# A hybrid decoder layer on one Trainium2 core: the second dilated pair and branch a take the logits of two query groups in one visit

## The chip, the cores and the metric

One core of one Trainium2 chip runs the whole layer. The metric is the device time of one execution in microseconds, the median of several runs. TensorE multiplies matrices into PSUM, of which the kernel uses eight banks; VectorE (DVE), ScalarE (ACT) and GpSimd (POOL) work on vectors; SyncE (SP) issues most of the loads. The program gives each engine its own list of instructions, which wait for those of other engines through semaphores.

## The reference

One layer, 256 tokens of width 1024, all float32. Three attention branches read one projection of x, and their outputs are merged under sigmoid gates:

```python
o_a = dsa_mixer(...)      # 6 heads share one key and value head; top-64 keys per query by an indexer
o_b = dilated_mixer(...)  # 3 query groups of 4 heads over shared keys and values
o_c = moba_mixer(...)     # 6 heads, causal within the one block of 256
gates = jax.nn.sigmoid(x @ w_gate[i]).reshape(bsz, s_len, N_BRANCH, D_MODEL)
merged = (gates[:, :, 0] * (o_a @ w_br_a[i]) + gates[:, :, 1] * (o_b @ w_br_b[i])
          + gates[:, :, 2] * (o_c @ w_br_c[i]))
x = layer_norm(ALPHA * x + merged @ w_out[i], ln1_g[i], ln1_b[i])
h = jnp.square(jax.nn.relu(x @ w_up[i])) @ w_down[i]
ple = jax.nn.sigmoid(x @ w_ple_gate[i]) * (p[i] @ w_ple[i])
x = layer_norm(ALPHA * x + h + ple, ln2_g[i], ln2_b[i])
```

Every head is softmax(q·k + bias + mask) times v. The bias is a table by distance; in branch a the mask comes from the top-64 selection.

## The kernel before

Float32 products are made of three matmuls: each operand is split into a high part of a shorter format and a low rest, and hi·hi, hi·lo and lo·hi are summed in PSUM (`prod`, line 189). For weights, `Weights._split` loads a unit into a `raw` buffer (SP), ACT casts its high part `whi` (line 112), DVE and POOL subtract to get `wlo` (lines 119 and 123). Buffers of `raw` and of the parts are five each, and units are split four ahead of their use, so a weight that is cast late also makes a later load late.

The first half of the program, up to about 198 us, computes the three branches. Its work is cut into units that the code interleaves:

- `feat(f)` makes 128 columns of queries or keys (24 matmuls of 128x256); `q_pair` and `k_pair` take the result out of PSUM.
- `fill("g")` makes one gate unit: 24 matmuls of 128x256 into a bank of the pool `mm` (three banks), then ACT's tanh at line 311 takes it out to `G`, and the bank is free.
- `fill("c")` makes one merge unit of branches b and c: 15 matmuls into an `mm` bank that read `op[:, 3..7]`, the outputs of five head pairs, then three DVE instructions (lines 326 and 327). A merge unit that lacks the output of one head pair keeps its bank until that output is there.
- `logits(k, *qs)` (line 347) makes the scores of the two heads of a query group: 12 matmuls that contract over 64 rows, the two heads on the two halves of the array, into one bank of `b0`, `b1`, `b2` for each head. Called with two groups, it makes 24 matmuls and takes four banks, the fourth being `b3` (`ps_t`), which the transposes of `attend` use otherwise. Before the change the first dilated pair and the indexer call it so.
- `head` (branches a and c) adds the bias and finds the row's extreme on DVE (line 416, two instructions, 128 and 256 columns), exps on ACT (line 419, two, each with a read of the accumulator), a reciprocal (DVE) and two scalings (ACT, line 408), then `attend`: three transposes on TensorE (line 388), two copies of the result (ACT line 389, DVE 390), two matmuls P·V (lines 392 and 393), ACT's copy `ov` (396), DVE's `ov` and `o` (397, 398). After the second head of a pair, `pair_out` casts the output to `op` (ACT 401, DVE 402).
- `slots` is the same for the three query groups of a dilated pair, with one softmax over all three.

Branch a has six heads in three pairs (j = 0, 1, 2). Before, each pair had its own q unit, its own logits visit and then its two heads one after the other; for each head POOL adds the bias table T and the selection mask `am` into `ta` (lines 584 and 585). Behind branch a come the last gate and merge units (`fill("gggcc")`), then the merge units of branch a, `merge(p)`, which read `op[:, 0..2]`. The list `TASKS` sets the order in which weight units are loaded and split. A scheduler orders the instructions within each engine from what the code says, so the same edit moves rows on all engines.

Of the kernel before, what the change touches and what calls it, by code (L numbers as in the profile page):

```python
# [11 lines left out]
F32 = mybir.dt.float32  # L12
F32R = mybir.dt.float32r
ALU = mybir.AluOpType
# [16 lines left out]
GONE = -3e38  # L31
# [10 lines left out]


TASKS = ("4 va 5 g 6 7 g 8 g g 9 g 10 11 g 12 g g vb g 13 14 g g 15 16 g g 17 18 g g "
         "19 g c 20 g c g c 21 g c g c g c g g g c c a a a a o o o o").split()


class Apart:
# [95 lines left out]
def hybrid_layer(ctx: ExitStack, tc: tile.TileContext, x0, xn, pT, wqk, wva, wvb, wg, wbc, wba,  # L144
                 wout, wup, wdn, wpg, wple, lnrow, rel, onehot, pick, out):
    nc = tc.nc
    pe, act, dve, pool = nc.tensor, nc.scalar, nc.vector, nc.gpsimd
# [17 lines left out]
    ps_s, ps_t, ps_v, ps_a = turns((0, 1, 2)), turns((3,)), turns((4,)), turns((0, 1, 3, 2, 4))  # L165
# [12 lines left out]
    t = banks.tile([128, 512], F32, name="b4", tag="b4")  # L178
# [28 lines left out]
    right = lambda n, b: one.enter_context(tc.tile_pool(name=n, bufs=b, side="right"))  # L207
# [23 lines left out]
    for t in TASKS:  # L231
# [4 lines left out]
        elif t in "gcao":  # L236
            u, w, n = {"g": (u_g, wg, 1024), "c": (u_bc, wbc, 640), "a": (u_ba, wba, 768),
                       "o": (u_out, wout, 1024)}[t]
# [26 lines left out]
    QC = (slice(0, 128), slice(128, 384))  # L265
# [16 lines left out]
    def q_pair(ps, scale=-0.125):  # L282

        q = qpool.tile([128, 2, S], F32R, name="q", tag="q")
        i = (act.mul(q[:, 0], ps, scale),
             dve.scalar_tensor_tensor(q[:, 1], ps, scale, q[:, 0].bitcast(F32), op0=ALU.mult,
                                      op1=ALU.subtract))
        freed(*i)
        last[:] = (x.ins for x in i)
        return q  # L290
# [38 lines left out]
    def feat(f):  # L329
        ps = mmbank(256)  # L330
        gemm(ps, u_q[f], xs)
        if f > 8:
            next(side, None)
        return ps

    def logits(k, *qs):


        ss = [next(ps_s if n < 3 else ps_t)[:, 0:384] for n in range(2 * len(qs))]
        with tc.high_priority(offset=500):  # L340
            for b in range(2):
                c = slice(b * 128, (b + 1) * 128)
                for n, q in enumerate(qs):
                    for i, (x, y) in enumerate(((1, 0), (0, 0), (0, 1))):
                        for h in (1, 0):
                            d = slice(64 * h, 64 * h + 64)
                            m = pe.matmul(ss[2 * n + h][:, QC[b]], lhsT=q[d, x, c],  # L347
                                          rhs=k[d, y, 0:128 * (b + 1)], start=i == 0, stop=i == 2)
                            if b or n or i or not h:
                                tc.keep_in_program_order(m)  # L350
        return ss
# [48 lines left out]
    def pair_out(o, kt):  # L400
        act.copy(op[:, kt, 0], o)
        dve.tensor_tensor(op[:, kt, 1], o, op[:, kt, 0].bitcast(F32), op=ALU.subtract)
# [5 lines left out]
            act.mul(P[:, QC[b]], P[:, QC[b]], r[:, b:b + 1])  # L408


    def head(s, t0, t1, vh, o, h):
        e = wk.tile([128, 384], F32, name="e", tag="e")
        mx = sm.tile([128, 2], F32, name="mx", tag="mx")
        den = sm.tile([128, 2], F32, name="den", tag="den")
        for b, t in enumerate((t0, t1)):
            dve.tensor_tensor_reduce(e[:, QC[b]], s[h][:, QC[b]], t, op0=ALU.add, op1=ALU.min,
                                     scale=1.0, scalar=-GONE, accum_out=mx[:, b:b + 1])
        for b in range(2):
            act.activation(e[:, QC[b]], e[:, QC[b]], AF.Exp, bias=mx[:, b:b + 1], scale=-1.0,
                           accum_out=den[:, b:b + 1])  # L420
        scale_rows(e, den)
        attend(e, vh, o, h)

    def slots(qs, k, Ts, vh, o, adds, two):

        es = [wk2.tile([128, 3, 384], F32, name="eb", tag="eb") for _ in range(2)]
        mxs = [sm.tile([128, 2, 3], F32, name="mxb", tag="mxb") for _ in range(2)]
        for g in range(3):

            if two and g == 0:  # L430
                s = logits(k, qs[1], qs[0])
                s, ss = s[2:], s[:2]
            else:
                s = ss if two and g == 1 else logits(k, qs[g])
            for h in range(2):
                for b, t in enumerate((Ts[h][:, g, 128:256], Ts[h][:, g, :])):
                    dve.tensor_tensor_reduce(es[h][:, g, QC[b]], s[h][:, QC[b]], t, op0=ALU.add,
                                             op1=ALU.min, scale=1.0, scalar=-GONE,
                                             accum_out=mxs[h][:, b, g:g + 1])
        for h in range(2):  # L440
            e = es[h]
            m = sm.tile([128, 2], F32, name="mx", tag="mx")
            den = sm.tile([128, 2], F32, name="den", tag="den")
            dve.tensor_reduce(m, mxs[h], axis=AX.X, op=ALU.min)
            for b in range(2):
                act.activation(e[:, :, QC[b]], e[:, :, QC[b]], AF.Exp, bias=m[:, b:b + 1],
                               scale=-1.0, accum_out=den[:, b:b + 1])
            adds.tensor_tensor(e[:, 0], e[:, 0], e[:, 1], op=ALU.add)
            adds.tensor_tensor(e[:, 0], e[:, 0], e[:, 2], op=ALU.add)
            scale_rows(e[:, 0], den)  # L450
            attend(e[:, 0], vh + h, o, h)
# [16 lines left out]
    with ExitStack() as begin:  # L468
# [7 lines left out]
        with tc.high_priority(offset=1000):  # L476
            for k in range(KT):
                for i, (a, b) in enumerate(cut[k]):
                    e = nc.scalar if i else nc.sync
                    e.dma_start(g0[:, k, a:b], x0[k, :, a:b])  # L480
            for k in range(KT):
                act.copy(xh[:, k], g0[:, k, 0:S])
                for a, b in cut[k]:
                    a = max(a, S)
# [7 lines left out]
                    pe.matmul(first[f], lhsT=w[:, k, 128 * f:128 * f + 128], rhs=x[:, k],  # L492
                              start=k == i == 0, stop=k == KT - 1 and i == 2)
        iq = [q_pair(ps, 0.125) for ps in first]
    tp, wk, wk2, sm = (right(n, b) for n, b in (("tp", 3), ("wk", 3), ("wk2", 2), ("sm", 6)))
    tab = bias_table()
    ps = feat(4)
    kI, kA = k_pair(ps[0:64], ps[0:64]), k_pair(ps[64:128], ps[64:128])
# [7 lines left out]

    values(u_va, 328, 0, 5, True)
    for j in range(4):
        s = s[2:] if j % 2 else logits(kI, iq[j], iq[j + 1])
        r = wk2.tile([128, 768], F32, name="ri", tag="eb")  # L510
        r = r.rearrange("p (h k) -> p h k", h=2)
        for h in range(2):
            act.activation(r[:, h], s[h], AF.Relu)
            n = 2 * j + h
            dve.scalar_tensor_tensor(idx[:, QC[1]], r[:, h, QC[1]], iw[:, 1, n:n + 1],
                                     idx[:, QC[1]], op0=ALU.mult, op1=ALU.add)
            act.mul(r[:, h, QC[0]], r[:, h, QC[0]], iw[:, 0, n:n + 1])  # L517
            pool.tensor_tensor(idx[:, QC[0]], idx[:, QC[0]], r[:, h, QC[0]], op=ALU.add)
# [14 lines left out]
    def opair():  # L533
        return wk2.tile([128, S], F32, name="o", tag="o")

    for j in range(2):
        ps = feat(5 + 4 * j)
        k = k_pair(ps)
        fill("g")
        qs = []  # L540
        for g in range(3):
            qs.append(q_pair(feat(6 + 4 * j + g)))
            if g:
                fill("g")
        o = opair()
        Ts = [toeplitz(6 + 2 * j + h, 4) for h in range(2)]
        slots(qs, k, Ts, 1 + 2 * j, o, (pool, dve)[j], j == 0)
        pair_out(o, 3 + j)
        banks_first[0] = True
        fill("g")  # L550
# [6 lines left out]
    for j in range(3):  # L557
        ps = feat(13 + 2 * j)
        k = k_pair(ps)
        q = q_pair(feat(14 + 2 * j))  # L560
        s = logits(k, q)
        o = opair()
        for h in range(2):
            n = 2 * j + h
            if n % 3 == 0:
                T = toeplitz(18 + n, 1)
            head(s, T[:, n % 3, 128:256], T[:, n % 3], 5 + n, o, h)
            fill("g")
        pair_out(o, 5 + j)

    for _ in side:
        pass
    T = None
    q = q_pair(feat(19))
    for j in range(3):
        s = logits(kA, q)
        o = opair()
        for h in range(2):
            n = 2 * j + h
            if n % 3 == 0:  # L580
                T = toeplitz(n, 1)
            ta = wk.tile([128, 384], F32, name="ta", tag="ta")
            with tc.issue_after(W.subs[-3]):
                pool.tensor_tensor(ta[:, 0:128], T[:, n % 3, 128:256], am[:, 0:128], op=ALU.add)
                pool.tensor_tensor(ta[:, 128:384], T[:, n % 3], am[:, 128:384], op=ALU.add)
            head(s, ta[:, 0:128], ta[:, 128:384], 0, o, h)
            if h and j < 2:
                q = q_pair(feat(20 + j))
            fill("gc")
        pair_out(o, j)  # L590
    fill("gggcc")
    W.after = ()

# [160 lines left out]
    for i in range(4):  # L754
# [3 lines left out]
        b, cs = i // 2, H[i % 2]  # L758
        t = slice(b * 128, (b + 1) * 128)
# [64 lines left out]
    for k in (*SEQ, *LATE):  # L824
        i = PAIRS.index(k) if k in PAIRS else -1
        n = 512 if i < 0 else 1792
# [11 lines left out]
    wr, wt = {}, {}  # L838
# [287 lines left out]
```

## Time and profile before

| what | value |
|---|---|
| runs of the kernel | 429.45 us median of 3 (429.26, 429.45, 430.65) |
| the profiled execution | 428.66 us |
| its span | 426.9 us |
| granted TensorE clock | 0.998 |
| instructions | 7810 |
| DVE busy | 351.1 us (82%) |
| POOL busy | 118.9 us (28%) |
| HBM read and written | 81.88 MB and 1.90 MB, 196 GB/s over the span |

The page gives each engine's busy time, the chain of work that ended last and the costliest groups; other views give single instructions with their start, duration and the wait ahead of them, or the busy time in a stretch of the span. Matmuls are pipelined: the record of a 128x256 matmul is some 0.28 us long, while one starts every 0.11 us, so costs on TensorE are read from start to start.

### The profile page before, as it was taken

How to read it: one execution, taken by the hardware profiler on the slowest of the kernel's cores; microseconds unless marked ns; L12 is line 12 of the kernel's file. 1: busy time of each engine (PE TensorE's matmuls, PEld its weight loads, DVE VectorE, ACT ScalarE, POOL GpSimd, SP SyncE). 2: the span in 40 equal slices, each digit the busy share in tenths (PEclk: the TensorE clock that was granted, in tenths of full speed). 3: DMA queues.
4: the chain of work that ended last, by engine and by line, in shares of the span. 5: the costliest groups of instructions: out<-in, count | busy, mean ns of one | idle time of the engine just before them, and what ended most of it. 6: DMA issues, size and time to landing. Idle time of an engine off the chain costs nothing.

```text
span 426.9 us, 7810 instructions
## 1 busy us (share of the span) xinstructions
PE 417.1 (98%) x2804; PEld 378.1 (89%) x2804; DVE 351.1 (82%) x645; ACT 279.6 (65%) x531; POOL 118.9 (28%) x127
## 2 busy tenths in 40 slices
PE   8999999999999999999999999999999999999993
PEld 8989999999999999999887888888888888788883
DVE  5968758898676689879967889989998798999755
ACT  6777385585888777858414668887888666567310
POOL 1668474173544556500010002242220000000001
PEclk9999999999999999999999999999999999999999
DMA  8895966567463327587851776785665376646402
GB/s 294 301 327 161 286 222 189 164 201 269 130 181 126 131 63 259 145 267 276 292 206 49 236 257 197 210 291 191 187 207 152 117 266 216 190 147 230 164 2 99
DMA packets 28157, 84.30 MB, mean 197 GB/s; under 512 B 2977, under 2 KB 6985, under 8 KB 27733
## 3 DMA queue, kind: packets, MB, share of 16 engines
q1 hardware_dynamic: 26880, 79.54, 57.0%
q10 hardware_dynamic: 1140, 4.19, 2.8%
q8 instruction: 22, 0.36, 0.4%
q14 instruction: 19, 0.15, 0.1%
q0 software_dynamic: 96, 0.06, 0.0%
HBM read 81.88 MB, written 1.90 MB: 196 GB/s over the span
## 4 chain that ended last, share of the span: by engine, by line
PE 78%; DVE 5%; DMA 4%; issue 2%; ACT 2%; SPq 0%; POOLq 0%; DVEq 0%; POOL 0%; ACTq 0%
PE mm L189 34%; PE b L189 19%; PE mm L891 14%; PE mm L893 7%; DMA xr<-in_wdn_dram 4%; PE b L347 2%; DVE wlo L119 2%; PE b L388 1%; PE b L392 1%; ACT whi L112 1%; DVE Y L853 1%; ACT ri L517 1%; PE b L393 0%; DVE wlo L123 0%; DVE st L701 0%
## 5 line engine op out<-in xcount | busy, mean ns | idle before, releaser
L112 ACT CAST whi<-raw 128x1024 fp32r<-128x1024 f32 (+3 forms) x92 | 89.9, 988 | 38.2 <-PE b L189 14.7
L123 DVE TENSOR_TENSOR wlo<-raw,whi 128x256 fp32r<-128x256 f32 (+3 forms) x118 | 96.4, 840 | 16.6 <-ACT whi L112 13.9
L189 PE MATMUL mm<-xh,whi 128*128 128x256 f32 x336 | 90.2, 280 | 0.0
L189 PE MATMUL mm<-xl,whi 128*128 128x256 f32 x336 | 88.1, 278 | 0.0
L123 POOL TENSOR_TENSOR wlo<-raw,whi 128x384 fp32r<-128x384 f32 (+1 forms) x50 | 68.4, 1377 | 70.2 <-ACT whi L112 65.5
L189 PE MATMUL mm<-xh,wlo 128*128 128x256 f32 x336 | 80.6, 281 | 0.2 <-DVE k L299 0.2
L189 PEld LDWEIGHTS mm<-xh,whi 128*128 128x128 f32 x336 | 63.1, 188 | 0.8
L891 PE MATMUL mm<-x,whi 128*128 128x512 f32 x256 | 63.4, 389 | 0.0
L189 PEld LDWEIGHTS mm<-xl,whi 128*128 128x128 f32 x336 | 63.1, 188 | 0.1
L189 PEld LDWEIGHTS mm<-xh,wlo 128*128 128x128 f32 x336 | 57.8, 188 | 0.8 <-DVE k L299 0.4
L189 PE MATMUL b<-whi,store 128*128 128x512 f32 x168 | 54.1, 389 | 0.0
L891 PEld LDWEIGHTS mm<-x,whi 128*128 128x128 f32 x256 | 45.7, 188 | 7.5
L119 DVE TENSOR_TENSOR wlo<-raw,whi 128x1024 fp32r<-128x1024 f32 (+2 forms) x38 | 43.2, 1159 | 3.7 <-ACT whi L112 3.6
L708 POOL TENSOR_TENSOR rs<-rs,half 128x1 f32<-128x1 f32 x4 | 3.4, 843 | 147.5 <-DVE rs L707 147.5
L110 ACT CAST whi<-raw 128x256 fp32r<-128x256 f32 x64 | 36.9, 617 | 10.0 <-PE mm L891 5.4
L189 PEld LDWEIGHTS b<-whi,store 128*128 128x128 f32 x168 | 31.5, 188 | 6.4
L893 PEld LDWEIGHTS mm<-x,wlo 128*128 128x128 f32 x256 | 33.8, 188 | 2.5
L893 PE MATMUL mm<-x,wlo 128*128 128x256 f32 x256 | 34.2, 276 | 0.0
L189 PE MATMUL b<-wlo,store 128*128 128x512 f32 x84 | 32.8, 391 | 0.3 <-DVE wlo L119 0.3
L914 POOL TENSOR_TENSOR a<-a 128x128 f32<-128x128 f32 x7 | 5.3, 757 | 61.5 <-ACT a L877 55.6
L189 PE MATMUL mm<-op,whi 128*128 128x256 f32 x128 | 22.4, 280 | 0.0
L189 PE MATMUL b<-whi,x 128*128 128x512 f32 x64 | 20.5, 395 | 0.0
(223 smaller groups left out, 824.2 us busy)
## 6 DMA issues: line engine op xcount, KB each, us to landing
raw<-in_wup_dram SPq DMA_DIRECT2D x32, 512.0 KB
raw<-in_wg_dram SPq DMA_DIRECT2D x24, 512.0 KB
raw<-in_wqk_dram SPq DMA_DIRECT2D x18, 512.0 KB
raw<-in_wdn_dram SPq DMA_DIRECT2D x18, 512.0 KB
raw<-in_wout_dram SPq DMA_DIRECT2D x8, 512.0 KB
raw<-in_wpg_dram SPq DMA_DIRECT2D x8, 512.0 KB
T<-tabd SPq DMA_DIRECT2D x24, 128.0 KB
xr<-in_wdn_dram SPq DMA_DIRECT2D x6, 512.0 KB
```

What stands on the lines that cost most here:

```text
L110: i = nc.scalar.copy(blocks(hi, a, b), blocks(r, a, b))
L112: i = nc.scalar.copy(hi, r)
L119: i = e.tensor_tensor(lo[:, x], r[:, x], hi[:, x].bitcast(F32), op=ALU.subtract)
L123: i = e.tensor_tensor(blocks(lo, *x), blocks(r, *x), blocks(hi, *x).bitcast(F32), op=ALU.subtract)
L189: i = pe.matmul(ps, lhsT=a[x], rhs=b[y], start=first and n == 0, stop=last and n == 2, skip_group_check=more)
L347: m = pe.matmul(ss[2 * n + h][:, QC[b]], lhsT=q[d, x, c], rhs=k[d, y, 0:128 * (b + 1)], start=i == 0, stop=i == 2)
L388: pe.transpose(t[:, 128 * i:128 * i + 128], P[:, 128 * i:128 * i + 128], ident)
L392: pe.matmul(v, lhsT=V[:, 0, vh], rhs=pt[:, :, 0:256], start=True, stop=False)
L517: act.mul(r[:, h, QC[0]], r[:, h, QC[0]], iw[:, 0, n:n + 1])
L891: pe.matmul(ps, lhsT=hi[:, c], rhs=x1[:, :, k], start=k == 0, stop=False)
L893: pe.matmul(ps[:, :, 0], lhsT=lo[:, c], rhs=x1[:, :, k, 0], start=False, stop=k == KT - 1)
L914: pool.tensor_tensor(sums[2], a11, a21, op=ALU.subtract)
```

## The change

The logits function takes pairs of key and query, and the second dilated pair (j = 1) and branch a (pairs 0 and 1) call it with two groups; the third pair of branch a keeps its own visit. With two groups it now takes the bank `b3` as its second bank (n == 1). `head` is cut in two: `biased` (the DVE part, bias and extreme) runs for all four heads of a visit first, then `head` for each. The buffer `ta` gets its own pool `wt` of three, and `wk` four buffers instead of three, so that four `e` tiles can be alive. Weight unit 20 is loaded ahead of one pair of gate and merge units.

```diff
-         "19 g c 20 g c g c 21 g c g c g c g g g c c a a a a o o o o").split()
+         "19 20 g c g c g c 21 g c g c g c g g g c c a a a a o o o o").split()
...
-    def logits(k, *qs):
-
-
-        ss = [next(ps_s if n < 3 else ps_t)[:, 0:384] for n in range(2 * len(qs))]
+    def logits(*kqs):
+
+        ss = [next(ps_t if n == 1 and len(kqs) == 2 else ps_s)[:, 0:384]
+              for n in range(2 * len(kqs))]
...
-    def head(s, t0, t1, vh, o, h):
+    def biased(s, t0, t1):
         e = wk.tile([128, 384], F32, name="e", tag="e")
         mx = sm.tile([128, 2], F32, name="mx", tag="mx")
+        for b, t in enumerate((t0, t1)):
+            dve.tensor_tensor_reduce(e[:, QC[b]], s[:, QC[b]], t, op0=ALU.add, op1=ALU.min,
+                                     scale=1.0, scalar=-GONE, accum_out=mx[:, b:b + 1])
+        return e, mx
+
+    def head(e, mx, vh, o, h):
         den = sm.tile([128, 2], F32, name="den", tag="den")
-        for b, t in enumerate((t0, t1)):
-            dve.tensor_tensor_reduce(e[:, QC[b]], s[h][:, QC[b]], t, op0=ALU.add, op1=ALU.min,
-                                     scale=1.0, scalar=-GONE, accum_out=mx[:, b:b + 1])
...
-    tp, wk, wk2, sm = (right(n, b) for n, b in (("tp", 3), ("wk", 3), ("wk2", 2), ("sm", 6)))
+    tp, wt, wk, wk2, sm = (right(n, b) for n, b in (("tp", 3), ("wt", 3), ("wk", 4), ("wk2", 2),
+                                                    ("sm", 6)))
...
-        slots(qs, k, Ts, 1 + 2 * j, o, (pool, dve)[j], j == 0)
+        slots(qs, k, Ts, 1 + 2 * j, o, (pool, dve)[j], True)
...
-    q = q_pair(feat(19))
-    for j in range(3):
-        s = logits(kA, q)
-        o = opair()
-        for h in range(2):
-            n = 2 * j + h
+    qs = [q_pair(feat(19 + j)) for j in range(2)]
+    for js in ((0, 1), (2,)):
+        ems = []
+        ss = logits(*((kA, q) for q in qs[::-1]))
+        for i, s in enumerate(ss[-2:] + ss[:-2]):
+            n = 2 * js[0] + i
             if n % 3 == 0:
                 T = toeplitz(n, 1)
-            ta = wk.tile([128, 384], F32, name="ta", tag="ta")
+            ta = wt.tile([128, 384], F32, name="ta", tag="ta")
...
-            head(s, ta[:, 0:128], ta[:, 128:384], 0, o, h)
-            if h and j < 2:
-                q = q_pair(feat(20 + j))
+            ems.append(biased(s, ta[:, 0:128], ta[:, 128:384]))
+        for i, em in enumerate(ems):
+            n = 2 * js[0] + i
+            if n % 2 == 0:
+                o = opair()
+            head(*em, 0, o, n % 2)
+            if n == 3:
+                qs = [q_pair(feat(21))]
             fill("gc")
-        pair_out(o, j)
+            if n % 2:
+                pair_out(o, n // 2)
     fill("gggcc")
```

How the rows of the engines move is shown at three places. Numbers behind a name tell buffers apart; `mm_` names the tile of a gate, merge or feature unit.

ACT at the first branch-a visit, before: two heads (`e_2175` and `e_2261`) and their scalings stand together, then a cast and a `q` that takes a feature unit out of PSUM.

```order
L396 COPY ov_2022<-b4_2019 64x512
L389 CAST pt1_116<-b3_2070 128x384
L419 ACTIVATE e_2175,den_2177<-e_2175,mx_2176 128x128
L419 ACTIVATE e_2175,den_2177<-e_2175,mx_2176 128x256
L419 ACTIVATE e_2261,den_2263<-e_2261,mx_2262 128x128
L419 ACTIVATE e_2261,den_2263<-e_2261,mx_2262 128x256
L408 ACTIVATE e_2175<-e_2175,r_2182 128x128
L408 ACTIVATE e_2175<-e_2175,r_2182 128x256
L408 ACTIVATE e_2261<-e_2261,r_2268 128x128
L408 ACTIVATE e_2261<-e_2261,r_2268 128x256
L112 CAST whi_2288<-raw_2286 128x640
L285 ACTIVATE q_2317<-mm_2285 128x256
```

ACT at the double visit of branch a, in the changed kernel: `ov_2082` belongs to the last head of branch c, the four `e` tiles to the four heads.

```order
L396 COPY ov_2082<-b4_2079 64x512
L422 ACTIVATE e_2226,den_2256<-e_2226,mx_2227 128x128
L422 ACTIVATE e_2226,den_2256<-e_2226,mx_2227 128x256
L422 ACTIVATE e_2233,den_2335<-e_2233,mx_2234 128x128
L422 ACTIVATE e_2233,den_2335<-e_2233,mx_2234 128x256
L422 ACTIVATE e_2240,den_2417<-e_2240,mx_2241 128x128
L422 ACTIVATE e_2240,den_2417<-e_2240,mx_2241 128x256
L112 CAST whi_2358<-raw_2356 128x1024
L311 ACTIVATE G_114<-mm_2355 128x256
```

Six exps and a cast of 1024 columns now stand between the copy `ov` and the tanh that frees the bank of the gate unit `mm_2355`. On TensorE the double visit stands in the middle of that gate unit's matmuls; behind it come the two matmuls P·V of the branch-c head, the 15 that are left of `mm_2355`, 12 of the merge unit `mm_2395`, and then the gate unit `mm_2437`, whose bank is the one that this tanh frees.

The rows that follow on ACT in the changed kernel, up to the next tanh:

```order
L422 ACTIVATE e_2251,den_2496<-e_2251,mx_2252 128x128
L408 ACTIVATE e_2226<-e_2226,r_2259 128x128
L408 ACTIVATE e_2226<-e_2226,r_2259 128x256
L422 ACTIVATE e_2251,den_2496<-e_2251,mx_2252 128x256
L401 CAST op_129<-o_2004 128x256
L408 ACTIVATE e_2233<-e_2233,r_2338 128x128
L408 ACTIVATE e_2233<-e_2233,r_2338 128x256
L408 ACTIVATE e_2240<-e_2240,r_2420 128x128
L408 ACTIVATE e_2240<-e_2240,r_2420 128x256
L408 ACTIVATE e_2251<-e_2251,r_2499 128x128
L408 ACTIVATE e_2251<-e_2251,r_2499 128x256
L112 CAST whi_2390<-raw_2388 128x1024
```

Behind the last of them stands the tanh of `mm_2437`; the exps of the fourth head, all eight scalings, `op` and a cast are ahead of it. TensorE goes from `mm_2437` (24 matmuls) over three transposes and six matmuls that close the merge units `mm_2316` and `mm_2395` to the merge unit `mm_2477`, which takes the bank of `mm_2437`.

DVE behind the last head of branch a, before: `ov_2733` and `o_2623` are the output of that head's P·V, `mm_2901` a merge unit of branches b and c.

```order
L397 TENSOR_TENSOR ov_2733<-b4_2730,ov_2733 64x512
L398 TENSOR_TENSOR o_2623<-ov_2733 64x256
L123 TENSOR_TENSOR wlo_2867<-raw_2864,whi_2866 128x6x128
L402 TENSOR_TENSOR op_129<-o_2623,op_129 128x256
L123 TENSOR_TENSOR wlo_2898<-raw_2895,whi_2897 128x6x128
L326 SCALAR_TENSOR_TENSOR mm_2901<-G_114,mm_2901 128x256
```

The same place in the changed kernel: `ov_2736` and `o_2640` are that head's output, `mm_2904` and `mm_2929` the last two merge units of branches b and c.

```order
L326 SCALAR_TENSOR_TENSOR mm_2904<-G_114,mm_2904 128x256
L326 SCALAR_TENSOR_TENSOR G_114<-G_114,mm_2904 128x256
L327 TENSOR_TENSOR G_114<-G_114,mm_2904 128x256
L123 TENSOR_TENSOR wlo_2926<-raw_2923,whi_2925 128x6x128
L397 TENSOR_TENSOR ov_2736<-b4_2733,ov_2736 64x512
L326 SCALAR_TENSOR_TENSOR mm_2929<-G_114,mm_2929 128x256
L119 TENSOR_TENSOR wlo_2970<-raw_2967,whi_2969 128x1024
L398 TENSOR_TENSOR o_2640<-ov_2736 64x256
L326 SCALAR_TENSOR_TENSOR G_114<-G_114,mm_2929 128x256
L327 TENSOR_TENSOR G_114<-G_114,mm_2929 128x256
L402 TENSOR_TENSOR op_129<-o_2640,op_129 128x256
```

The head's P·V moved behind the last gate units, into the last merge unit `mm_2929`, and on DVE its `ov` and `o` moved between the splits of the next weights. On TensorE, ten matmuls of `mm_2929` and twelve of `merge(p)` stand between P·V and the first matmul that reads `op[:, 2]`, the output of this head pair.

More of the change, by code (lines that the diff above doesn't have):

```diff
@@ L342, in logits @@
                 c = slice(b * 128, (b + 1) * 128)
-                for n, q in enumerate(qs):
+                for n, (k, q) in enumerate(kqs):
                     for i, (x, y) in enumerate(((1, 0), (0, 0), (0, 1))):
@@ L430, in slots @@
             if two and g == 0:
-                s = logits(k, qs[1], qs[0])
+                s = logits((k, qs[1]), (k, qs[0]))
                 s, ss = s[2:], s[:2]
             else:
-                s = ss if two and g == 1 else logits(k, qs[g])
+                s = ss if two and g == 1 else logits((k, qs[g]))
             for h in range(2):
@@ L508, in hybrid_layer @@
     for j in range(4):
-        s = s[2:] if j % 2 else logits(kI, iq[j], iq[j + 1])
+        s = s[2:] if j % 2 else logits((kI, iq[j]), (kI, iq[j + 1]))
         r = wk2.tile([128, 768], F32, name="ri", tag="eb")
@@ L560, in hybrid_layer @@
         q = q_pair(feat(14 + 2 * j))
-        s = logits(k, q)
+        s = logits((k, q))
         o = opair()
@@ L566, in hybrid_layer @@
                 T = toeplitz(18 + n, 1)
-            head(s, T[:, n % 3, 128:256], T[:, n % 3], 5 + n, o, h)
+            head(*biased(s[h], T[:, n % 3, 128:256], T[:, n % 3]), 5 + n, o, h)
             fill("g")
```

## The prediction

> **What bounds the kernel now.** I read the page's busy shares first, then the chain that ended last, then the stretches in which the changed code runs.
>
> ```profile
> PE 417.1 (98%) x2804; PEld 378.1 (89%) x2804; DVE 351.1 (82%) x645; ACT 279.6 (65%) x531; POOL 118.9 (28%) x127
> PE 78%; DVE 5%; DMA 4%; issue 2%; ACT 2%; SPq 0%; POOLq 0%; DVEq 0%; POOL 0%; ACTq 0%
> ```
> ```profile
> 140.00:160.00 20.00, 19.75 (x173) 18.76 (x173) 14.39 (x39) 15.85 (x38) 10.58 (x11) 1.00 0.30 98
> 160.00:180.00 20.00, 20.00 (x176) 19.59 (x176) 18.22 (x47) 15.85 (x38) 12.94 (x13) 1.00 0.60 201
> 180.00:200.00 20.00, 20.00 (x167) 19.58 (x167) 17.67 (x30) 13.25 (x20) 0.00 (x0) 1.00 0.83 280
> 200.00:220.00 20.00, 20.00 (x90) 16.57 (x89) 16.69 (x25) 7.13 (x11) 0.74 (x1) 1.00 0.82 292
> ```
> The columns of the windows are the length, then the busy time of PE, PEld, DVE, ACT and POOL, the granted clock, the DMA share and GB/s. TensorE has no idle time where branch a runs (about 140 to 186 us) except 0.25 us, at a granted clock of 1.00. So a matmul that starts later there, later by d, ends the kernel later by d, and one saved microsecond of TensorE is one saved of the kernel. ACT is busy 15.85 of 20 us: it is near its own limit, which matters below.
>
> ```profile
> PE b L180 <- POOL ident masks.py:199: 1.7, 1, 1.7
> PE b L189 <- DVE wlo L119: 0.3, 1, 0.3
> PE mm L189 <- DVE wlo L123: 0.3, 1, 0.3
> PE mm L189 <- DVE k L299: 0.2, 1, 0.2
> ```
> These are all of TensorE's waits on other engines. One lies in the changed stretch, that on wlo L123:
>
> ```profile
> 155.68 0.49 PE L388 MATMUL b<-ident,e 128*128 128x128 f32 x3
> 155.97 0.51 PE L189 MATMUL mm<-op,whi 128*128 128x256 f32 x2
> 156.72 0.50 PE L189 MATMUL mm<-op,wlo 128*128 128x256 f32 x2 [0.25 <-DVE wlo L123]
> ```
> The two matmuls of 155.97 take 0.51 us together and a plain one 0.28 (the row of 48.19 below), so the second starts at 156.20; the next was due at 156.31 and came at 156.72: 0.4 us are lost. The three transposes ahead occupy 155.97 - 155.68 = 0.29 us.
>
> **What the change takes off TensorE.** No matmul is added or removed; two visits of 12 logits matmuls become one of 24, once in the second dilated pair and once in branch a.
>
> ```profile
> 46.07 0.39 PE L189 MATMUL mm<-xh,wlo 128*128 128x256 f32 x2
> 46.39 1.64 PE L347 MATMUL b<-k,q 64*128 64x128 f32 x24
> ...
> 48.19 0.28 PE L189 MATMUL mm<-xl,whi 128*128 128x256 f32 x1
> ...
> 78.86 0.28 PE L189 MATMUL mm<-xl,whi 128*128 128x256 f32 x1
> 79.06 0.96 PE L347 MATMUL b<-k,q 64*128 64x128 f32 x12
> ...
> 80.17 0.28 PE L189 MATMUL mm<-xh,whi 128*128 128x256 f32 x1
> ```
> ```profile
> 183.36 14.70 PE mm L189 x129
> ```
> A plain matmul costs 14.70/129 = 0.114 us. From the last one before a visit to the second one behind it are two plain steps, 0.23 us, and the visit. The single visit: 80.17 - 78.86 - 0.23 = 1.08 us. The double one that the kernel already has (the second of the two matmuls of 46.07 starts at 46.07 + 0.11 = 46.18): 48.19 - 46.18 - 0.23 = 1.78 us. Two singles for one double save 2.16 - 1.78 = 0.38 us, twice in the kernel: **-0.76 us**. The lost 0.4 us at 156.72 should go too: in the new order the low words that the merge units of branches b and c use stand on VectorE well ahead of their matmuls. **-0.4 us**; if it stays, the sum is 0.4 higher.
>
> The third dilated group, the T loads that SP issues in a changed order, the pool of their own for ta and the weight unit that is loaded one gate unit earlier I cost at nothing: they lie beside the full TensorE stream, and the smallest margin that I find there is about 0.7 us, ahead of the first matmul that waits for V. If that cover goes, 0 to 0.5 us.
>
> **What the change adds: two waits behind a burst on ACT.** Before, ACT serves one or two heads between two gate units; now the exps of three heads stand in a row, ahead of a cast and of the tanh that frees a PSUM bank.
>
> ```profile
> 142.78 0.40 ACT L419 ACTIVATE e<-e,mx 128x128 f32<-128x128 f32 x1
> 143.08 0.19 ACT L419 ACTIVATION_READ_ACCUMULATOR e<-e,mx 128x1 f32 x1
> ...
> 144.55 1.48 ACT L408 ACTIVATE e<-e,r 128x128 f32<-128x128 f32 x4
> 145.94 0.71 ACT L112 CAST whi<-raw 128x640 fp32r<-128x640 f32 x1
> ...
> 148.88 1.05 ACT L112 CAST whi<-raw 128x1024 fp32r<-128x1024 f32 x1 [0.25 <-PE mm L189]
> 149.83 0.38 ACT L311 ACTIVATE G<-mm 128x256 f32<-128x256 f32 x1
> 150.11 0.40 ACT L401 CAST op<-o 128x256 fp32r<-128x256 f32 x1
> 150.40 0.40 ACT L419 ACTIVATE e<-e,mx 128x128 f32<-128x128 f32 x1
> ```
> From start to start: four exps 144.55 - 142.78 = 1.77 us (0.44 each), four scalings 145.94 - 144.55 = 1.39 us (0.35 each), the cast of 1024 0.95 us, the tanh 0.28 (0.38 until done), the cast of op 0.29.
>
> ```profile
> 182.85 0.40 PE L392 MATMUL b<-pt,V 128*128 128x512 f32 x1
> 183.20 0.28 PE L189 MATMUL mm<-xh,whi 128*128 128x256 f32 x1
> 183.40 0.58 ACT L396 COPY ov<-b 64x512 f32<-64x512 f32 x1 [1.68 <-PE b L393]
> 184.00 0.38 ACT L311 ACTIVATE G<-mm 128x256 f32<-128x256 f32 x1
> ```
> The two matmuls of a head's P·V take 0.35 us, and ACT's copy ov starts 0.55 us behind the first and occupies 0.60.
>
> *First wait.* Take the start of the double visit of branch a as 0. TensorE does the visit (1.78), P·V of the last branch-c head (0.35) and 27 plain matmuls (3.08), and stands at 5.21 before the first matmul of the gate unit mm_2437. Its bank is the one that tanh of mm_2355 frees; the other two banks hold merge units that still wait for the output of that last head. ACT: ov from 2.33 to 2.93, six exps to 5.59, the cast of 1024 to 6.54, the tanh done at 6.92. **+1.7 us**, and every instruction on TensorE stands behind it. Bounds: 1.2 if an exp takes the 0.35 of a scaling; 2.3 if the accumulator's reads of 0.19 us, of which some 0.1 lies beside the next exp now, hide nothing. I take the spacing of the rows, since it is the same pair of operations in the same order.
>
> The Trainium skill, ScalarE: Activation LUTs (What ACT_TABLE_LOAD costs), gives an ACTIVATE with a pointer bias about 280 ns + 0.833 ns per column and lets two in a row overlap by 93 ns; an estimate by it is 0.35 us for a mean exp and 1.2 us for this wait, a sum about 0.8 lower with the two exps ahead of the next one. The trace has the accumulator's read of 0.19 us between the exps and 0.44 us from one to the next, so the rows decide.
>
> *Second wait.* TensorE goes on at 6.92: 24 matmuls of that unit (2.74), three transposes (0.29), six matmuls that close the two merge units (0.68): 10.63 at the first matmul of mm_2477, which needs the bank of mm_2437. ACT, from 6.82: two exps 0.88, two scalings 0.70, op 0.29, six scalings 2.09, the cast of 1024 0.95, the tanh 0.38: 12.11. **+1.5 us** (1.1 with such short exps and the transposes at their full 0.49; 1.8 with unhidden reads and op at its full 0.40).
>
> **And a third wait, behind the last head.** Its P·V moves from ahead of a whole gate unit and two merge units to the middle of the last merge unit of branches b and c. Before, P·V is at 182.85; now only 22 plain matmuls lie between it and the first that reads its output.
>
> ```profile
> 184.01 0.68 DVE L397 TENSOR_TENSOR ov<-b,ov 64x512 f32<-64x512 f32 x1 [1.01 <-ACT ov L396]
> 184.73 0.42 DVE L398 TENSOR_TENSOR o<-ov 64x256 f32<-64x256 f32 x1
> 185.18 0.41 ACT L401 CAST op<-o 128x256 fp32r<-128x256 f32 x1
> ...
> 188.54 0.42 DVE L326 SCALAR_TENSOR_TENSOR mm<-G,mm 128x256 f32<-128x256 f32 x1
> ...
> 189.79 0.95 DVE L123 TENSOR_TENSOR wlo<-raw,whi 128x768 fp32r<-128x768 f32 x1
> 190.66 0.42 DVE L326 SCALAR_TENSOR_TENSOR mm<-G,mm 128x256 f32<-128x256 f32 x1
> 190.99 1.22 DVE L119 TENSOR_TENSOR wlo<-raw,whi 128x1024 fp32r<-128x1024 f32 x1
> ```
> With P·V at 0, TensorE is there at 0.35 + 22 x 0.114 = 2.86. VectorE first ends the three instructions on the merge unit before (189.79 - 188.54 = 1.25; that unit's last matmul is the sixth ahead of P·V, so they begin at about -0.68 + 0.28 = -0.40): 0.85; wlo of 768 (190.66 - 189.79 = 0.87) to 1.72; ov, 0.68, to 2.4; L326 (190.99 - 190.66 = 0.33) to 2.7; wlo of 1024, which the new order puts between ov and o, to 3.9; o 0.42 to 4.3; ACT's cast of op 0.41 to 4.75. **+1.9 us** (1.6 if all of these overlap by the 0.08 us that wlo of 768 and the next row do; 2.2 at full durations). What follows on TensorE waits for the same VectorE rows and comes within 0.2 us.
>
> **The sum**: -0.76 - 0.4 + 1.7 + 1.5 + 1.9 = +3.9 us. The profiled execution took 428.66 us (span 426.9), so its like would take 432.6. It lies 0.8 below the median of the three runs, 429.45; against that the sum gives **433.4 us**, +0.9%. Within 0.3% (1.29 us, about what a measurement of this kernel can tell) is 428.2 to 430.7.
>
> **Rivals.**
> *The stalls are given back.* Place: the stretch behind 200 us. If transfers set the end there, and not TensorE, then TensorE would be waiting for weights anyway, and five microseconds of wait near 165 and 190 us would let loads run ahead. For it speaks a DMA share of 0.82 at 200 to 220; against it, that TensorE is busy 20.00 of 20 there, and that its only waits for weights sum to 0.6 us. It decides from the point where the later waits are worth the 5.1 us that I add. It would leave between -1.16 and 0: 428.3 to 429.5, not slower. A tenth.
> *Only some of the waits come.* The first goes if the tanh ends before 5.21, for which the six exps and the cast must take under 1.9 us where the rows give 3.6; the second then starts ACT earlier by as much and shrinks too. The third has its own cause on VectorE. With two of the three, 3.3 us, the sum is -1.16 + 3.3 = +2.1 (431.5), a tenth; with one, 1.7, it is +0.5 (429.9), a tenth.
> *More than the three.* The casts that ACT does late free raw buffers late, and SP issues its loads in order: if a weight load is then late for its cast, another 1 to 2 us, 434.4 and up. For it: SP's loads wait for casts of buffers five units back; against: the DMA share there is 0.30 to 0.60, and the waits themselves give the loads 3 us more. 0.06.
>
> **The numbers.** All three waits: the lower bounds give 1.2 + 1.1 + 1.6 - 1.16 = +2.7 (432.2), the upper ones 2.3 + 1.8 + 2.2 + 0.2 - 0.76 = +5.7 (435.2): 0.64. Two, 431.5: 0.10. One, 429.9: 0.10, within 0.3%. Given back: 0.10, half faster and half within. More: 0.06. So slower 0.80, same 0.15, faster 0.05. The range takes the first three cases: 429.7 to 435.2.
>
> **What would show it.** Right: in TensorE's waits, mm on ACT G L311 twice with over 1 us each, about 5 and 12 us behind a logits group of x24, and mm on the cast of op (L401) once with over 1.3 us just behind the last P·V; two groups of x24 more and four of x12 fewer. The exps and the cast stand on ACT back to back between ov and the tanh. Wrong: TensorE busy 20.00 of 20 in all these stretches; the waits there, but the up and down projections shorter by as much; or a wait on DMA raw that I don't have.

## The result, and the profile after

| | before | after |
|---|---|---|
| median of the runs | 429.36 us (4 runs) | 435.27 us (4 runs: 434.29, 435.01, 435.54, 436.34) |
| profiled execution | 428.66 us | 434.29 us |
| its span | 426.9 us | 432.5 us |

The ratio is 1.0135 [1.0113, 1.0157]: the changed kernel is slower, by 5.9 us between the medians and by 5.63 between the profiled executions. Forecast were +3.9 and 433.4 us, with 435.2 as the end of the range; the median lies just above that end.

The page's busy shares of the changed kernel, then its windows over the stretches that were read before:

```profile
PE 418.0 (97%) x2804; PEld 378.7 (88%) x2804; DVE 354.2 (82%) x645; ACT 279.4 (65%) x531; POOL 116.9 (27%) x127
```
```profile
140.00:160.00 20.00, 17.30 (x155) 16.56 (x154) 11.36 (x37) 15.35 (x40) 7.23 (x8) 1.00 0.27 84
160.00:180.00 20.00, 20.00 (x177) 19.62 (x176) 18.61 (x43) 14.37 (x31) 13.77 (x13) 1.00 0.63 199
180.00:200.00 20.00, 17.90 (x151) 17.40 (x150) 14.66 (x27) 9.76 (x17) 0.46 (x1) 1.00 0.74 231
200.00:220.00 20.00, 19.49 (x100) 16.34 (x100) 18.86 (x26) 12.62 (x18) 0.00 (x0) 1.00 0.79 255
```
The work is the same (2804 matmuls, busy times equal within 1%, POOL's within 2%), so the time is lost between instructions. Before, TensorE was idle 0.25 us from 140 to 220; now it is idle 2.70, 2.10 and 0.51 us in three of the four stretches, 5.3 us in all. Its waits on other engines name them (the engine and line waited for, then the sum, the number of waits and the longest):

```profile
PE mm L189 <- ACT G L311: 2.7, 2, 1.5
PE mm L189 <- ACT op L401: 2.1, 1, 2.1
...
PE b L189 <- DVE store L677: 0.5, 1, 0.5
```
Two waits on the tanh (G, L311) and one on the cast of `op` (L401) are the three that were forecast. The wait on `store` was not.

**The first two waits.** ACT's rows of the changed kernel at branch a's double visit, as start, duration and instruction:

```profile
147.91 0.58 ACT L396 COPY ov<-b 64x512 f32<-64x512 f32 x1 [3.50 <-PE b L393]
148.40 0.40 ACT L422 ACTIVATE e<-e,mx 128x128 f32<-128x128 f32 x1
148.70 0.19 ACT L422 ACTIVATION_READ_ACCUMULATOR e<-e,mx 128x1 f32 x1
148.79 0.50 ACT L422 ACTIVATE e<-e,mx 128x256 f32<-128x256 f32 x1
...
151.05 1.03 ACT L112 CAST whi<-raw 128x1024 fp32r<-128x1024 f32 x1
152.10 0.38 ACT L311 ACTIVATE G<-mm 128x256 f32<-128x256 f32 x1
...
156.34 1.04 ACT L112 CAST whi<-raw 128x1024 fp32r<-128x1024 f32 x1
157.27 0.38 ACT L311 ACTIVATE G<-mm 128x256 f32<-128x256 f32 x1
```
and TensorE's rows that come behind them, with the idle time ahead in brackets:

```profile
145.68 1.64 PE L347 MATMUL b<-k,q 64*128 64x128 f32 x24
147.25 0.51 PE L392 MATMUL b<-pt,V 128*128 128x512 f32 x1
...
152.53 0.38 PE L189 MATMUL mm<-xh,wlo 128*128 128x256 f32 x1 [1.53 <-ACT G L311]
...
157.71 0.50 PE L189 MATMUL mm<-op,whi 128*128 128x256 f32 x2 [1.16 <-ACT G L311]
```
Six exps stand between `ov` and the cast: 151.05 - 148.40 = 2.65 us, 0.44 each. TensorE starts 0.05 us behind the tanh's end at 152.48. The idle time of a row counts from the end of the matmul ahead, whose record is 0.28 us where its step is 0.114, so what is lost is the idle time and 0.17 us: **1.70 us** at 152.53 and **1.33 us** at 157.71 (forecast 1.7 and 1.5). The matmul behind each of them then starts 0.22 us later in place of 0.114 (0.50 - 0.28 in the row of 157.71), which is another 0.11 us each; this is called the wide step below. The estimate that the prediction made by the Trainium skill, ScalarE: Activation LUTs (What ACT_TABLE_LOAD costs), 0.35 us for an exp and a first wait of 1.2 us, does not agree with these rows: 0.44 and 1.70.

**The third wait.** VectorE, ACT and TensorE behind the last head's P·V, which stands at 190.66 on TensorE:

```profile
189.74 0.96 DVE L123 TENSOR_TENSOR wlo<-raw,whi 128x768 fp32r<-128x768 f32 x1 [1.11 <-ACT whi L112]
190.61 0.42 DVE L326 SCALAR_TENSOR_TENSOR mm<-G,mm 128x256 f32<-128x256 f32 x1
...
192.73 0.68 DVE L397 TENSOR_TENSOR ov<-b,ov 64x512 f32<-64x512 f32 x1
193.33 0.41 DVE L326 SCALAR_TENSOR_TENSOR mm<-G,mm 128x256 f32<-128x256 f32 x1
193.66 1.21 DVE L119 TENSOR_TENSOR wlo<-raw,whi 128x1024 fp32r<-128x1024 f32 x1
194.90 0.42 DVE L398 TENSOR_TENSOR o<-ov 64x256 f32<-64x256 f32 x1
...
195.35 0.41 ACT L401 CAST op<-o 128x256 fp32r<-128x256 f32 x1 [1.98 <-DVE o L398]
...
195.81 0.97 PE L189 MATMUL mm<-op,whi 128*128 128x256 f32 x4 [2.10 <-ACT op L401]
```
The order on VectorE is the forecast one, ov, L326, wlo of 1024, o. The wait costs 2.10 + 0.17 = **2.27 us** (forecast 1.9). And the four matmuls that follow it need 0.97 us, (0.97 - 0.28)/3 = 0.23 from start to start in place of 0.114: another 0.35 us, which the prediction put at within 0.2. Two of these steps are wide ones; between them the third matmul, at 196.28, waits for VectorE's `G` of L327, done at 196.22.

### The profile page after: what moved, and what is told of

Same layout as the page of the kernel before. It is cut to its first block, busy times and chain, and to the rows that moved or that the text cites. A ratio compares the mean times of both kernels' runs of the same rounds, so it can differ in the third digit from the quotient of the medians.

```text
span 432.5 us, 7803 instructions
## 1 busy us (share of the span) xinstructions
PE 418.0 (97%) x2804; PEld 378.7 (88%) x2804; DVE 354.2 (82%) x645; ACT 279.4 (65%) x531; POOL 116.9 (27%) x127
## 4 chain that ended last, share of the span: by engine, by line
PE 57%; DVE 3%; issue 2%; POOLq 0%; ACT 0%; DVEq 0%; POOL 0%
PE b L189 23%; PE mm L901 13%; PE mm L189 12%; PE mm L903 7%; DVE store L119 1%; DVE wlo L119 1%; DVE G L671 1%; PE b L388 0%; DVE st L711 0%; PE b L392 0%; DVE G L672 0%; PE mm L752 0%; POOLq L1132 0%; DVE store L677 0%; PE b L347 0%
## 5 line engine op out<-in xcount | busy, mean ns | idle before, releaser
L123 DVE TENSOR_TENSOR wlo<-raw,whi 128x256 fp32r<-128x256 f32 (+3 forms) x118 | 99.4, 865 | 18.9 <-ACT whi L112 15.9
L123 POOL TENSOR_TENSOR wlo<-raw,whi 128x384 fp32r<-128x384 f32 (+1 forms) x50 | 66.6, 1339 | 69.1 <-ACT whi L112 64.6
L189 PEld LDWEIGHTS mm<-op,whi 128*128 128x128 f32 x128 | 19.0, 188 | 4.0 <-ACT op L401 2.3
```

The source lines that it names most:

```text
L123: i = e.tensor_tensor(blocks(lo, *x), blocks(r, *x), blocks(hi, *x).bitcast(F32), op=ALU.subtract)
L189: i = pe.matmul(ps, lhsT=a[x], rhs=b[y], start=first and n == 0, stop=last and n == 2, skip_group_check=more)
```

## The experiments

Ten kernels follow. The kernel before was run beside each of them on the same chip; its median was 429.36 us beside the first four, 429.0 beside the fifth and the last, and 429.46 beside the others. Each ratio is to the one beside it.

**One half at a time.** First the second dilated pair alone, in the code of before:

```diff
-        slots(qs, k, Ts, 1 + 2 * j, o, (pool, dve)[j], j == 0)
+        slots(qs, k, Ts, 1 + 2 * j, o, (pool, dve)[j], True)
```

> The kernel before with one edit: the second dilated pair takes two query groups in one visit; branch a is as before. If the loss comes from the order around branch a (theory): TensorE saves one visit, 0.4 to 0.6 us, and no wait on a tanh or on op over 0.5 us appears: 428.8 to 429.1 us, within 0.3% of before. If the dilated pair carries part of the loss (rival): 430.5 or more. The start of the projection may come up to 0.9 us later or earlier than in the profile of before, as it did in the changed kernel; that belongs to neither.

430.09 us, ratio 1.0015 [1.0001, 1.0028]: neither. Its TensorE rows say why:

```profile
70.81 0.55 PE L347 MATMUL b<-k,q 64*128 64x128 f32 x6
...
75.31 1.31 PE L347 MATMUL b<-k,q 64*128 64x128 f32 x18
...
103.03 0.50 PE L392 MATMUL b<-pt,V 128*128 128x512 f32 x1 [0.46 <-DVE pt L390]
```
The instructions were put in another order with the buffers of before. The visit of 24 is cut into 6 and 18, and a P·V that had no wait now waits for `pt`. So this run doesn't show what the visit of the changed kernel, which is whole, is worth; a comparison of the profiles matmul by matmul does, in the section on the prediction.

Second, branch a alone, in the code of after:

```diff
-        slots(qs, k, Ts, 1 + 2 * j, o, (pool, dve)[j], True)
+        slots(qs, k, Ts, 1 + 2 * j, o, (pool, dve)[j], j == 0)
```

> The changed kernel with the second dilated pair as before. Theory: it keeps all three waits in the same places (mm on the tanh twice, 1.4 to 1.8 us each; mm on the cast of op, 2.1 us) and lacks one merged visit: 0.4 to 0.6 us above the changed kernel, about 435.8. Rival (the dilated part carries some of the loss): below 434.5.

435.62 us, ratio 1.0142 [1.0117, 1.0167], the whole loss of the change, with the same waits on G (2.7 us in two) and on op (2.1 us). It also has a wait of 0.4 us on `pt` in the dilated pair that the changed kernel has not. One more thing was new. Windows of its profile behind the third wait, with the granted clock as the third number from the end:

```profile
196.00:198.00 2.00, 1.06 (x4) 1.03 (x5) 1.59 (x4) 0.41 (x1) 0.00 (x0) 0.76 0.85 252
198.00:200.00 2.00, 2.00 (x11) 2.00 (x11) 0.00 (x0) 0.00 (x0) 0.00 (x0) 0.50 0.85 315
200.00:202.00 2.00, 2.00 (x17) 2.00 (x17) 0.77 (x2) 0.81 (x1) 0.00 (x0) 0.89 0.81 326
```
For some 3.4 us the clock is half and a matmul takes 0.21 us: 11 in 2 us where the next windows have 20. The profile of after had the same wait and clock 1.00 in all these windows.

**Taking the waits away.** Third, the changed kernel with its gate and merge units emitted earlier among the heads, one pair of them ahead of the second head, none behind the last (`q` of pair 2 moves with them):

```diff
-            if n == 3:
+            if n == 2:
                 qs = [q_pair(feat(21))]
-            fill("gc")
+            fill(("gcgc", "gc", "gc", "gc", "gc", "")[n])
```

> The changed kernel with the gate and merge units of branch a emitted one head earlier. On ACT the six exps and the two tanhs stand as in the changed kernel, but the last head's P.V stands 37 instead of 22 matmuls ahead of the first that reads its output. Theory (three separate waits): the two waits on the tanh stay (1.7 and 1.4 us), the wait on op falls from 2.3 by 15 x 0.114 = 1.7 us to under 0.8: 433 to 434. Rival (the third wait is a consequence of the first two, or given back elsewhere): the time stays at 435.

431.44 us, ratio 1.0043 [1.0028, 1.0057]. Its waits, apart from those on `ident` and `k` that the kernel before has too, come down to one line:

```profile
PE mm L189 <- ACT G L311: 2.7, 2, 1.5
```
Both waits on G are as before; those on op and on store are gone. The last P·V now stands 32 matmuls ahead of the next one that is held up, not 22. That is 3.1 to 3.8 us less than the changed kernel (434.58 and 435.27), more than was expected of that wait alone. Matmul by matmul, the third wait and what follows it fall from 2.6 us to 0.8, which two short waits for VectorE leave there; the wait on store goes (0.8 us), and this profile has no stretch at half clock.

Fourth, that kernel with, in addition, each head of branch a issued behind the tanh that was emitted before it, so that the tanh doesn't queue behind the exps of later heads:

```diff
-                freed(act.activation(G[:, n_g[0]], ps, AF.Tanh, scale=0.5))
+                tanhs.append(freed(act.activation(G[:, n_g[0]], ps, AF.Tanh, scale=0.5)))
...
-            head(*em, 0, o, n % 2)
+            with ExitStack() as held:
+                held.enter_context(tc.issue_after(tanhs[-1]))
+                head(*em, 0, o, n % 2)
```

> As the run before it, and on ACT each head of branch a stands behind the tanh of the gate unit emitted ahead of it, so that no more than one head's exps lie between two tanhs of the double visit. Logits visit, bias of four heads ahead and all buffers are those of the changed kernel. Theory: both waits on the tanh go (3.1 us) and the third is as in the run before: 429 to 430.7. Rival (the loss is that of four biased heads or of the larger buffers, not of the order on ACT): 433 or more.

429.86 us, ratio 1.0014 [1.0003, 1.0025]. Its waits on G, 2.7 us in two before, are down to one of 0.3 us:

```profile
PE mm L189 <- ACT G L311: 0.3, 1, 0.3
```
So all but some 0.5 us of the loss comes from ACT's order and from the place of the last P·V. That the merged visits' saving doesn't show is due to five waits of 0.2 to 0.5 us that are left on TensorE between 145 and 200 us, 2.0 us in all with the wide step behind each.

Fifth, tanh's order without the earlier units (the second edit alone, on the changed kernel):

> The changed kernel with each head of branch a issued behind the tanh emitted before it, and the gate units where the change put them (the run with earlier units and tanh first came to 429.86 us). If the first two waits are tanh standing behind the exps and the cast on ScalarE, both fall from 1.7 and 1 us to under 1 us. If the third wait is a matter of VectorE's work behind a late P.V of the last head, it depends on how many matmuls lie between that P.V and its use: it stays at 1 us or more if they stay 22, and goes if more of them now lie there. 430 to 431.5 if it goes too, 432 to 433.5 if it stays.

430.74 us, ratio 1.0041 [1.0029, 1.0053]. ACT's rows:

```profile
149.94 0.50 ACT L422 ACTIVATE e<-e,mx 128x256 f32<-128x256 f32 x1
...
150.43 1.03 ACT L112 CAST whi<-raw 128x1024 fp32r<-128x1024 f32 x1
151.49 0.38 ACT L311 ACTIVATE G<-mm 128x256 f32<-128x256 f32 x1
151.77 0.39 ACT L422 ACTIVATE e<-e,mx 128x128 f32<-128x128 f32 x1
```
Two of the six exps now stand behind the tanh, and its wait is lower by about their 0.88 us; the waits on G are 1.1 us in two. The wait on op is gone here too, since the order that results has the last P·V at 187.48, 36 matmuls ahead of the next one that is held up: the third wait follows from where the heads end. What is left at that place, as in the third and the fourth kernel, are two short waits for VectorE, here in the rows of the weight loads (PEld):

```profile
192.21 0.30 PEld L189 LDWEIGHTS mm<-op,whi 128*128 128x128 f32 x2 [0.30 <-DVE G L327]
...
193.41 0.19 PEld L189 LDWEIGHTS mm<-op,whi 128*128 128x128 f32 x1 [0.32 <-DVE op L402]
```
With the wide step behind each they cost 0.8 us.

**VectorE's order at the third wait.** The changed kernel with `o` ahead of the wlo of 1024:

```diff
-        dve.tensor_tensor(o[64 * h:64 * h + 64], x[:, 0], x[:, 1], op=ALU.add)
+        i = dve.tensor_tensor(o[64 * h:64 * h + 64], x[:, 0], x[:, 1], op=ALU.add)
+        last[0] = i.ins
...
+    o_last = last[0]
     fill("gggcc")
-    W.after = ()
+    W.after = (o_last,)
```

> The changed kernel, except that the 128x1024 wlo subtraction is issued on VectorE behind the last head's o instead of between its ov and o (an order edit only; the same instructions). If the third wait, 2.1 us on the cast of op, is that o stands behind wlo's 1.21 us, it shrinks to 0.9 to 1.2 us. The first matmul that takes op low then waits some 0.4 to 1 us more, since wlo is now ahead of that, so that the profiled span comes out 0.4 to 1.2 us shorter than that of the changed kernel (432.5 us), and the two waits on G stay at 1.7 and 1 us. And if it is the length of the third wait that lets the granted clock drop to half in some executions, no stretch at half clock appears near 200 us, and the median falls by more, to 432.8 to 434.3. The rival, that VectorE's order there is of no account because the last P.V comes late: the wait stays at about 2 us, 435 or so.

433.52 us, ratio 1.0100 [1.0086, 1.0113]; the changed kernel itself, run beside it, had 434.58 (below). Its waits:

```profile
PE mm L189 <- DVE op L403: 1.0, 1, 1.0
PE mm L189 <- ACT op L402: 1.0, 1, 1.0
```
(Its lines stand one further down: L402 makes op's high half, L403 the low one.) The wait on the high half is halved, and the other half comes back on the low one, 2.0 us together as before: VectorE has the same work to do ahead of that point, in either order. But this profile has neither a window near 200 us with a clock under 1.00 nor a wait on store, and the 1.06 us gained beside the changed kernel are of that size.

**The changed kernel once more.**

> The changed kernel once more, word for word, for a second profiled execution: does a stretch at half clock follow the wait of 2.1 us on op? If it does in some executions and not in others, the profiled times of this kernel fall into two groups some 1.4 us apart, 434.3 and 435.5 to 436; if the clock never drops in it, the profiled time is again 434.3 and the median of the timed runs is above it for another reason.

434.58 us (434.26, 434.58, 434.58, 435.61), ratio 1.0131 [1.0115, 1.0147]. The windows of its profile:

```profile
196.00:198.00 2.00, 2.00 (x15) 2.00 (x14) 0.00 (x0) 0.00 (x0) 0.00 (x0) 0.66 0.77 274
198.00:200.00 2.00, 2.00 (x11) 2.00 (x11) 0.89 (x2) 0.92 (x1) 0.00 (x0) 0.50 0.92 358
200.00:202.00 2.00, 2.00 (x19) 2.00 (x19) 2.00 (x3) 1.25 (x3) 0.00 (x0) 0.99 0.26 107
```
This time the stretch is there, and no wait on store behind it; the kernel with branch a alone had both. Two clear groups of times did not appear. The first loads, which differ from run to run as well (by 0.66 us between the two profiles of this kernel, last section), may be what blurs them.

**The half that saves, without the half that costs.** The changed kernel with branch a in three single visits, weight unit 20 loaded where it was before, and tanh first:

```diff
-         "19 20 g c g c g c 21 g c g c g c g g g c c a a a a o o o o").split()
+         "19 g c 20 g c g c 21 g c g c g c g g g c c a a a a o o o o").split()
...
-    qs = [q_pair(feat(19 + j)) for j in range(2)]
-    for js in ((0, 1), (2,)):
+    qs = [q_pair(feat(19))]
+    for js in ((0,), (1,), (2,)):
...
-            if n == 3:
-                qs = [q_pair(feat(21))]
+            if n in (1, 3):
+                qs = [q_pair(feat(20 + n // 2))]
```

> The part of the change that saves, without the part that costs: the second dilated pair in one visit, branch a in three visits as before, and each head of branch a issued behind the tanh emitted before it. If branch a's merged visit is what brings the waits on G and op, none over 0.6 us is left between 145 and 200 us, and the dilated visit's saving of 0.3 to 0.5 us less the wait on pt of 0.7 us (seen with the pair alone) nets to zero: 428.6 to 429.8, the time of before. The rival, that the four merged dilated heads are themselves a loss further on: 430 or more.

**428.28 us, ratio 0.9974 [0.9964, 0.9983]**: better than both kernels, and than was expected, since the wait on `pt` doesn't come. The double visit is whole here:

```profile
75.60 1.64 PE L347 MATMUL b<-k,q 64*128 64x128 f32 x24
...
156.70 0.51 PE L189 MATMUL mm<-op,wlo 128*128 128x256 f32 x2 [0.19 <-DVE wlo L123]
```
and the wait on wlo of the kernel before stays, at 0.19 us. Two kernels split this gain. With single visits in the dilated pair too (the slots call with `j == 0`):

> No merged visit at all, but each head of branch a issued behind the tanh emitted before it, so that tanh does not queue behind exps in the kernel before either (its wait of 0.4 us at 156.72). If that wait was a real loss and is not given back behind 200 us, the time is 0.3 to 0.8 us below the kernel before: 428.5 to 429.1. The rival, that it is taken up by a later wait: within 0.2 us of the kernel before.

429.29 us, ratio 0.9999 [0.9989, 1.0009], no difference. But it isn't clean: with the new buffers and no double visit of the second pair, VectorE does the first dilated pair in another order, and the profile has a wait there that the kernel before has not:

```profile
PE b L392 <- DVE pt L390: 0.5, 1, 0.5
```
So what tanh's order alone is worth in the code of before stays open. And with the double visit but without tanh first:

> The kernel with the dilated pair in one visit and branch a in three, without the order given to tanh: what of its 428.28 us is due to that order? If the merged dilated visit alone carries the gain, 428.0 to 428.8. If tanh's order matters with single visits too, TensorE shows a wait of 0.5 to 1 us on G near 156 us, and the time is 428.9 to 429.6.

430.30 us, ratio 1.0027 [1.0015, 1.0038], above both expectations. ACT's tanh in that kernel and, in the second fence, in the one with 428.28 us:

```profile
151.68 0.50 ACT L422 ACTIVATE e<-e,mx 128x256 f32<-128x256 f32 x1
...
156.25 0.38 ACT L311 ACTIVATE G<-mm 128x256 f32<-128x256 f32 x1
```
```profile
151.76 0.58 ACT L396 COPY ov<-b 64x512 f32<-64x512 f32 x1 [0.35 <-PE b L393]
...
155.67 0.38 ACT L311 ACTIVATE G<-mm 128x256 f32<-128x256 f32 x1
...
156.88 0.40 ACT L422 ACTIVATE e<-e,mx 128x128 f32<-128x128 f32 x1
```
The exps of the second head of a visit stand ahead of the tanh in one and behind it in the other, 0.58 us for the tanh. What follows are small waits, all for VectorE: on G of L327, wlo of L123 and twice pt of L390, and none on the tanh. By the two ratios, tanh's order is worth 0.5% there; how the second head's exps lead to waits for VectorE is not shown.

## Why the prediction was nearly right

- **Direction and mechanism: right.** The three waits came at the forecast places, with the forecast rows in the forecast order, and two groups of 24 logits stand where four of 12 were. The fifth and the fourth kernel confirm the cause of the first two, ACT's exps and cast ahead of the tanh.
- **First and second wait: right.** 1.70 us measured for 1.7, 1.33 for 1.5. The spacing of 0.44 us for an exp, taken from the rows of before, held. The sum left out the wide step behind each, 0.11 us.
- **Third wait: the mis-sized term.** 2.27 us for 1.9, and 0.35 behind it where "within 0.2" stood. Its rows begin later than worked out: VectorE had `ov` at 192.73, 2.07 us behind P·V, where the prediction had 1.72. It let the three instructions on the merge unit begin when that unit's last matmul is done, 0.40 us ahead of P·V; in fact VectorE was then still at a wlo of 768 (the row of 189.74, which had waited 1.11 us for ACT's cast), and they began at 190.61, 0.05 us ahead. Nor does the wait hang on VectorE's rows alone ("has its own cause on VectorE"): in the third kernel, where both waits on the tanh stay, and in the fifth, where tanh's order is the only edit, it goes down to 0.8 us, because the last P·V stands further ahead of its use.
- **Savings: somewhat larger.** When the start of each matmul, counted from the first, is compared with the start of the same number in the profile of before, TensorE gains 0.54 us at the dilated visit and 0.53 at that of branch a, for 0.38 each. The stall at 156.72 gives 0.56, with the wide step behind it, for 0.4.
- **Not foreseen: the wait on store and the half clock.** In the profiled execution 0.8 us are lost behind 208 us, where VectorE, already delayed, delivers `store` (L677) late:

```profile
208.22 2.36 DVE L119 TENSOR_TENSOR store<-raw,store 128x1024 fp32r<-128x1024 f32 x2
210.49 0.76 DVE L677 SCALAR_TENSOR_TENSOR store<-G,store 128x256 fp32r<-128x256 f32 x2
```
  This is the reverse of the rival "given back": beyond 200 us a later stall (at 370 us) shortens by only 0.34 us, and a new one of 0.8 comes. In the second profile of the changed kernel the stretch at half clock comes instead, in that of branch a alone both come. Nothing in the sum stood for the clock; between 4 and 400 us TensorE has no idle time of 2 us in the profile of before, so it couldn't be read there.
- **Costed at nothing: held, as far as it can be seen.** The T loads, ta's pool and weight unit 20 leave no wait of their own in the changed kernel, and the fourth kernel, which has them all, is within 0.14% of the one before.
- **The bridge to the median.** The profiled execution of before was 0.7 us below the median of 429.36, and its first loads came earlier than in any other profile here; in that of after they came 0.85 us later. So of the 5.63 us between the two profiles 0.85 are no part of the change. The rest adds up as 1.81 + 1.44 for the first two waits with their wide steps, 2.62 for the third and what follows it and 0.80 behind 208 us, less 0.54, 0.53, 0.56 and 0.34: 4.7 us, where the sum had 3.9. Between the medians, 435.27 and 434.58 against 429.36 and 429.46, the change costs 5.1 to 5.9 us.

## What to carry to other kernels

A merged visit saves half a microsecond of a full TensorE by itself, but it bunches what the visit feeds: count, on each engine behind it, what now stands ahead of the instruction that frees the next PSUM bank, and give that instruction its place before merging. When several waits follow one burst, test the order of the burst first; removing one instruction from ahead of the last wait (o ahead of wlo) only moved the same wait to the next result. And an experiment that makes "one half of the change" can be given another order by the scheduler: look at the group sizes in its trace before reading its time.

## What the hardware showed that was not expected

*A stretch at half clock behind 2.1 us of idle time.* In two of three profiles with the wait of 2.1 us on op, the granted clock was half for about 3.4 us from shortly behind it (the windows of 0.76, 0.50, 0.89 and of 0.66, 0.50, 0.99), and in the third it stayed at 1.00. With 11 matmuls per 2 us in place of 20, 3.4 us at half clock cost about 1.5 us. The wait of 1.53 us at 152.53 is followed by full clock in all of these, and no 2-us window up to 420 us in the other ten profiles has a clock under 1.00. The Trainium skill, TensorE: Matmul & The Clock Gate (What's actually happening), has the clock halved after at least one idle window of about 3.4 us, in windows that run freely. The length of the stretch and its chance appearance agree with that; the idle time that was enough here, 2.1 us, does not.

*The first loads.* ACT's second cast of x waits for its load, after (first fence) and before:

```profile
6.94 0.41 ACT L485 CAST xh<-G 128x256 fp32r<-128x256 f32 x1 [1.16 <-DMA G<-in_x_dram]
```
```profile
6.48 0.41 ACT L482 CAST xh<-G 128x256 fp32r<-128x256 f32 x1 [0.66 <-DMA G<-in_x_dram]
```
This code is the same in all kernels; 20 us into the span, TensorE was 0.2 to 1.2 us later than in the profile of before in the other profiles. A comparison of two single profiles carries that much.
